# Identity matmuls behind the steps of a delta-rule chain

## The chip, the core and the metric

The kernel runs on one core of one Trainium2 chip. The metric is the device time of one execution, in microseconds. The core has five engines with queues of their own, each of which takes its instructions in the order written: TensorE (PE in the profile, with its weight loads as PEld), VectorE (DVE), ScalarE (ACT), GpSimd (POOL) and SyncE (SP), which here issues the DMAs.

## The reference

The reference is a trunk of four layers over a sequence of 1024 tokens with 1024 channels. The layers' mixers are a gated short convolution (layers 0 and 3), a diagonal state-space scan (layer 1) and RWKV-7 time mixing (layer 2). The change concerns layer 2 alone. Its core is a recurrence over tokens for 16 heads of 64 channels:

```python
def _rwkv_step(state, inp):
    r_t, w_t, k_t, v_t, kk_t, a_t = inp
    sa = jnp.einsum("bhvk,bhk->bhv", state, -kk_t)
    state = (state * w_t[:, :, None, :] + sa[..., None] * (kk_t * a_t)[:, :, None, :]
             + v_t[..., None] * k_t[:, :, None, :])
    out = jnp.einsum("bhvk,bhk->bhv", state, r_t)
    return state, out
```

Around it stand the projections of r, k, v and z, a normalisation by head, and an output projection; each layer ends with a gate and a layer norm.

## The kernel before, in words

Activations lie with channels on the 128 partitions and tokens along the row, in two halves of 512 tokens (h = 0 and 1, "first" and "second half" in this text). Large projections run as three matmuls with a high and a low part of each operand (`mm3`, lines 326 to 328), over eight blocks of 128 input channels: 24 matmuls of 512 columns into one PSUM bank. Their outputs come from the pool `pmm`, which has three banks in this layer. Weights arrive by DMA (L295) and are split by ScalarE (L298) and VectorE (L299).

In the delta-rule layer, channels go in eight pairs of heads, m0 to m7, for each half. The recurrence is done in chunks of 64 tokens, eight chunks to a half. For each pair there are these parts:

- the projection of k and `use_k` (L1708 on), the projection of r and `use_r` (L1750 on): scaling, decay and norms, on all engines;
- `prep`: products within a chunk (L1982, `s`), masks on VectorE, copies on ScalarE, transposes (L2006), more small matmuls (L2017);
- `tsolve`: a triangular solve on VectorE (L2037 to L2054);
- `join`: what the solve gave is brought into the chain's operands (L2076 to L2109);
- `seq`: the chain itself, eight steps that follow each other, and behind them the output with its normalisation (L2141 on).

One step of `seq` is a matmul of the state into a partial sum (L2127), a copy of 64 rows of it by ScalarE (L2128), a second matmul with that copy (L2131), and two instructions on VectorE that decay the state and add the result (L2134). The next step's first matmul needs the new state. All matmuls of the chain are plain fp32 of 128 columns; the trace has two records for each.

The parts are Python generators. Their instructions are written by `pull` between those of the projections: while pair m is projected and prepared, `tsolve` of the pair before and `seq` of the pair before that one are pulled. Besides, a scheduler reorders instructions by priority and readiness when the program is built; `prio` gives `seq`, `tsolve`, `prep` and `join` a priority ahead of their place in the code. So the order on each engine comes from code, priorities and free buffers together. The layer's first half ends with m7, then the projections of the second half's z and v come (about 160 us), then the second half's eight pairs.

Of the kernel before, what the change touches and what calls it, by code (L numbers as in the profile page):

```python
# [8 lines left out]
F32 = mybir.dt.float32  # L9
# [6 lines left out]
P = 128  # L16
NB = 8
T = 1024
HT = 512
# [922 lines left out]
def rsqrt(S, t, y, v):  # L942

    V = S.nc.vector
    V.tensor_scalar(y.bitcast(I32), v.bitcast(I32), -0.5, float(0x5f3759df), ALU.mult, ALU.add)
    V.tensor_scalar(v, v, -0.5, None, ALU.mult)
    for _ in range(3):
        if v.shape[-1] == 1:
            V.scalar_tensor_tensor(t, y, v, y, ALU.mult, ALU.mult)
        else:  # L950
            V.tensor_tensor(t, y, y, ALU.mult)
            V.tensor_tensor(t, t, v, ALU.mult)
        V.scalar_tensor_tensor(y, t, 1.5, y, ALU.add, ALU.mult)
# [574 lines left out]
    w_out_res(S, ("ssm_w_out", (0,)), y2, resid, "b")  # L1528


DECAY = math.exp(-0.5)
GN_EPS = 64e-5
NC = 16
# [52 lines left out]
def rsqrt_small(S, pool, dst, v, n, V):  # L1586

    nc = S.nc
    t = pool.tile([P, n], F32, tag=f"rs_t{n}", name="rs_t", bufs=2)
    nc.scalar.activation(t, v, AF.Ln)  # L1590
    nc.scalar.activation(dst, t, AF.Exp, scale=-0.5)
    V.tensor_tensor(t, dst, dst, ALU.mult)
    V.tensor_tensor(t, t, v, ALU.mult)
    V.tensor_scalar(t, t, -0.5, 1.5, ALU.mult, ALU.add)
    V.tensor_tensor(dst, dst, t, ALU.mult)


def rwkv_layer(S, X, bg, l, last, nxt):
# [102 lines left out]
    def use_k(m, h, ps, R):  # L1701
# [4 lines left out]
        G.memset(pt[:, :, 0:1], 1.0)  # L1706
        SC.activation(pt[:, :, 1:], c3(cs), AF.Exp, scale=-DECAY)
        SC.activation(cs, cs, AF.Exp, scale=DECAY)  # L1708
        R.pc = rg.tile([P, 8], F32, tag="pc", name="pc", bufs=5)
# [212 lines left out]
def inner_setup(S, rg, T_):  # L1922
    nc = S.nc
# [30 lines left out]
    def sq(nm):  # L1954
        return S.pseq.tile([P, HT], F32, tag="sq", name=nm)
# [158 lines left out]
    def seq(m, h, R, dVT, dST, dBV, dZ, dY):  # L2114
        st = rg.tile([P, P], F32, tag="state", name="state", bufs=2)
        if h == 0:
            G.memset(st, 0.0)
        else:
            nc.sync.dma_start(st, dST[m][:])
        ot = S.tmp.tile([P, HT], F32, tag="t_u", name="o")  # L2120
        o4 = ot.rearrange("p (c s) -> p c s", c=4)
        for c in range(8):
            w, c2 = c % 2, c // 2
            rb = rows_b[w]
            uv = R.uv[w][:, c2, :]
            p1 = R.p1[w][:, c2, :]
            nc.tensor.matmul(p1, R.ra[:, c, :], st, start=False, stop=False, skip_group_check=True)  # L2127
            SC.copy(uv[rb, :], p1[rb, :])  # L2128
            yield
            p2 = sq("p2")  # L2130
            last = nc.tensor.matmul(p2[:, 0:P], R.kbt[c // 4][:, c % 4, :], uv, start=True, stop=True)  # L2131
            for hd in range(2):
                cs = slice(hd * 64, hd * 64 + 64)
                V.scalar_tensor_tensor(st[cs, cs], st[cs, cs], R.pc[cs, c:c + 1], p2[cs, cs], ALU.mult, ALU.add)  # L2134
            yield
        with S.tc.issue_after(last.ins):
            for c2 in range(4):
                for hd in range(2):
                    for w in range(2):
                        cs = slice(hd * 64, hd * 64 + 64)  # L2140
                        nc.tensor.matmul(R.p1[w][rows_k[w], c2, cs], R.scr[w][:, c2, hd, :], R.uv[w][:, c2, cs],  # L2141
                                         start=False, stop=True, skip_group_check=True)
        for w in range(2):
            SC.copy(o4[rows_k[w]], R.p1[w][rows_k[w]])
        if h == 0:
            nc.sync.dma_start(dST[m][:], st)

        hs = slice(h * HT, (h + 1) * HT)
        o = ot.rearrange("p (g v) -> p g v", v=64)
        s1 = rg.tile([P, 8], F32, tag="gn_s", name="gn_s", bufs=2)  # L2150
        s2 = rg.tile([P, 8], F32, tag="gn_q", name="gn_q", bufs=2)
        bcs = lambda t: t.unsqueeze(2).to_broadcast([P, 8, 64])
        gsq = S.tmp.tile([P, 8, 64], F32, tag="t_u", name="gsq")
        for g in range(8):
            SC.activation(gsq[:, g, :], o[:, g, :], AF.Square, scale=0.125, accum_out=s2[:, g:g + 1])
        G.tensor_scalar(s2, s2, GN_EPS, None, ALU.add)
        yield
        if m == NB - 1:
            rsqrt(S, rg.tile([P, 8], F32, tag="rs_t8", name="rs_t", bufs=2), s1, s2)
        else:  # L2160
            rsqrt_small(S, rg, s1, s2, 8, V)
        G.tensor_tensor(o, o, bcs(s1), ALU.mult)
        bv = S.tmp.tile([P, HT], F32, tag="ln_s", name="bv", bufs=1)
        nc.sync.dma_start(bv, dBV[m][:, hs])
        z = S.tmp.tile([P, HT], F32, tag="ln_v", name="zz", bufs=1)
        nc.sync.dma_start(z, dZ[m][:, hs])
        ps = sq("otp")
        for i in range(4):
            nc.tensor.transpose(ps[:, i * P:(i + 1) * P], ot[:, i * P:(i + 1) * P], S.ident)
        yt = S.tmp.tile([P, HT], F32, tag="t_u", name="yt")  # L2170
        q4 = lambda ap: ap.rearrange("p (c w t) -> p c w t", w=2, t=CH)
        SC.activation(q4(yt), q4(ps)[:, :, ::-1, :], AF.Identity, scale=gn[:, m:m + 1], bias=bn[:, m:m + 1])
        G.tensor_tensor(yt, yt, bv, ALU.add)
        G.tensor_tensor(yt, yt, z, ALU.mult)
        nc.sync.dma_start(dY[m][:, hs], yt)
        yield
# [29 lines left out]
```

## Time and profile before

| What | Value |
|---|---|
| Runs shown | 2845.06, 2836.07, 2841.19 us |
| Median | 2841.19 us |
| Profiled execution | 2839.38 us, of which the span from first to last instruction 2837.7 us |
| Mean granted clock of TensorE | 0.963 |
| Delta-rule sequences, first half | from 1350.5 us to 1661.0 us |
| Delta-rule sequences, second half | from 1822.7 us to 2109.9 us |

The table of the page gives each engine's busy time and share of the span. Its line PEclk gives the clock granted to TensorE in 40 slices, in tenths of full speed. A row of busy time by stretch reads: start and end, length, then for PE, PEld, DVE, ACT and POOL the busy time and (x) the instructions, then the mean granted clock, the share of time that the DMA engines were busy, and GB/s. A row of the timeline reads: start, length, engine, line, operation, output<-inputs, shape and count; in brackets the idle time of the engine before it, and whose work ended that.

### The profile page before, as it was taken

What the parts mean: (1) busy time and instruction counts of PE and PEld (TensorE: products, weight loads), DVE (VectorE), ACT (ScalarE), POOL (GpSimd) and SP (SyncE); (2) the same over time, 40 slices, a digit from 0 to 9 for tenths busy, and PEclk for the clock granted to TensorE, in tenths of its full rate; (3) what the DMA queues carried; (4) which work ended last, traced back from release to release, by engine and by line L of the source; (5) the groups of instructions that cost most, each with busy time, mean ns of one, the idle gap of its engine ahead of it and who ended that gap; (6) DMA issues with size and microseconds to landing.
All of it is one profiled execution on the core that took longest, in us unless ns stands there. A gap on an engine that the chain in (4) does not pass through costs nothing.

```text
span 2837.7 us, 40655 instructions
## 1 busy us (share of the span) xinstructions
PE 2681.3 (94%) x14939; PEld 2127.4 (75%) x14939; DVE 1994.8 (70%) x3584; ACT 1163.1 (41%) x2211; POOL 646.9 (23%) x696
## 2 busy tenths in 40 slices
PE   8999999999999999899888799898889999999998
PEld 6877788778877888576667567666768777887887
DVE  6787865477657346888888667888756678876544
ACT  3333322242135223656555476555534343224332
POOL 1143422221116132203333110333232211111000
PEclk9999999999999999999997799999699999999999
DMA  5333322347884333473222245223234433324511
GB/s 168 98 97 97 95 75 66 89 142 212 220 240 140 104 94 122 117 233 107 78 85 87 63 151 170 84 91 89 78 100 135 144 111 111 108 71 129 171 64 38
DMA packets 463128, 331.56 MB, mean 117 GB/s; under 512 B 49449, under 2 KB 398929, under 8 KB 462929
## 3 DMA queue, kind: packets, MB, share of 16 engines
q1 hardware_dynamic: 462928, 328.96, 38.3%
q8 instruction: 118, 1.93, 0.3%
q14 instruction: 82, 0.66, 0.1%
HBM read 250.77 MB, written 77.59 MB: 116 GB/s over the span
## 4 chain that ended last, share of the span: by engine, by line
PE 70%; DVE 16%; ACT 4%; issue 4%; DMA 3%; POOL 3%; SPq 0%; DVEq 0%; POOLq 0%; ACTq 0%
PE op L327 3%; PE op L326 3%; PE op L328 3%; PE gp L328 3%; PE gp L327 3%; PE gp L326 3%; PE sp L326 3%; PE sp L327 3%; PE sp L328 2%; DVE tv L2048 2%; PE qa L508 2%; PE qa L506 2%; PE qa L507 2%; PE zp L326 2%; PE zp L328 2%
## 5 line engine op out<-in xcount | busy, mean ns | idle before, releaser
L299 DVE TENSOR_TENSOR wl<-wraw,wh 128x1024 fp32r<-128x1024 f32 x255 | 331.1, 1299 | 217.9 <-ACT wh L298 214.2
L298 ACT CAST wh<-wraw 128x1024 fp32r<-128x1024 f32 x255 | 267.5, 1049 | 517.7 <-PE gp L327 191.5
L905 POOL TENSOR_TENSOR ln_s<-ln_s,rp 128x512 f32<-128x512 f32 x42 | 60.0, 1429 | 209.8 <-DVE rp L901 209.8
L2134 DVE SCALAR_TENSOR_TENSOR state<-state,pc,p 64x64 f32<-64x64 f32 x256 | 71.1, 278 | 46.9 <-PE p L2131 42.1
L2048 DVE TENSOR_TENSOR tv<-ti,mi 128x128 f32<-128x128 f32 (+3 forms) x128 | 97.8, 764 | 2.4
L2127 PE MATMUL p<-state,ra 128*128 128x128 f32 x256 | 65.6, 343 | 28.8 <-DVE state L2134 26.7
L2128 ACT COPY uv<-p 64x128 f32<-64x128 f32 x128 | 33.1, 259 | 136.5 <-PE p L2127 135.8
L2127 PEld LDWEIGHTS p<-state,ra 128*128 128x128 f32 x256 | 45.8, 217 | 54.1 <-DVE state L2134 44.0
L1982 PEld LDWEIGHTS s<-ra,kb 64*128 64x128 f32 x512 | 64.7, 213 | 20.4 <-ACT scr L1988 6.2
L1982 PE MATMUL s<-ra,kb 64*128 64x128 f32 x512 | 75.2, 314 | 4.1 <-DVE kb L1738 1.9
L328 PE MATMUL gp<-r_0h,wl 128*128 128x512 f32 x192 | 77.5, 404 | 0.0
L327 PE MATMUL gp<-r_0l,wh 128*128 128x512 f32 x192 | 76.8, 400 | 0.0
L326 PE MATMUL gp<-r_0h,wh 128*128 128x512 f32 x192 | 76.6, 399 | 0.0
L326 PE MATMUL gp<-r_1h,wh 128*128 128x512 f32 x192 | 76.4, 398 | 0.0
L920 POOL TENSOR_TENSOR rp<-r_0h,r_0l 128x512 f32<-128x512 f32 x24 | 36.3, 1544 | 174.9 <-PE op L327 174.9
L328 PE MATMUL gp<-r_1h,wl 128*128 128x512 f32 x192 | 76.1, 396 | 0.1
L2131 PE MATMUL p<-uv,kbt 128*128 128x128 f32 x256 | 66.8, 347 | 9.9 <-ACT uv L2128 9.8
L327 PE MATMUL gp<-r_1l,wh 128*128 128x512 f32 x192 | 75.6, 394 | 0.0
L2131 PEld LDWEIGHTS p<-uv,kbt 128*128 128x128 f32 x256 | 44.5, 212 | 37.7 <-ACT uv L2128 31.9
L1991 POOL TENSOR_TENSOR scr<-scr,mask 128x512 f32<-128x512 f32 x32 | 46.0, 1436 | 55.4 <-ACT scr L1988 55.2
L326 PE MATMUL sp<-xs0h,wh 128*128 128x512 f32 x128 | 56.1, 438 | 2.6 <-DVE aq L1720 2.2
L327 PE MATMUL sp<-xs0l,wh 128*128 128x512 f32 x128 | 56.0, 437 | 1.9 <-DVE xs0l L195 1.9
(851 smaller groups left out, 8669.6 us busy)
## 6 DMA issues: line engine op xcount, KB each, us to landing
wraw<-in_conv_w_in_dram SPq DMA_DIRECT2D x84, 512.0 KB
wraw<-in_rwkv_w_rkvz_dram SPq DMA_DIRECT2D x64, 512.0 KB
wraw<-in_ple_gate_dram SPq DMA_DIRECT2D x56, 512.0 KB
wraw<-in_conv_w_out_dram SPq DMA_DIRECT2D x24, 512.0 KB
xt<-xd SPq DMA_DIRECT2D x48, 256.0 KB
wraw<-in_ssm_w_in_dram SPq DMA_DIRECT2D x21, 512.0 KB
xd<-rp SPq DMA_DIRECT2D x40, 256.0 KB
wraw<-in_rwkv_w_out_dram SPq DMA_DIRECT2D x16, 512.0 KB
```

Source lines behind the costliest of these rows:

```text
L298: nc.scalar.copy(wh, raw)
L299: nc.vector.tensor_tensor(wl, raw, f32(wh[:]), ALU.subtract)
L326: nc.tensor.matmul(ps, lh, xh, start=(n == 0), stop=False)
L327: nc.tensor.matmul(ps, lh, xl, start=False, stop=False)
L328: nc.tensor.matmul(ps, ll, xh, start=False, stop=(n == kt - 1))
L506: nc.tensor.matmul(ps, wh[:, k0 + k, :], xh, start=first and k == 0, stop=False, skip_group_check=True)
L905: nc.gpsimd.tensor_tensor(s, s, rs, ALU.add)
L1982: nc.tensor.matmul(pss[hd][:, c * P:(c + 1) * P], kb[rows, 2 * c + w, :], ra[rows, 2 * c + w, :], start=True, stop=True)
L2048: V.tensor_tensor(tv, ti[:, b:8, 4 * b:4 * b + 4].unsqueeze(2).to_broadcast([P, n, c, 4]), mi[:, 4 * b:4 * b + 4, 0:c].rearrange("p q c -> ...
L2127: nc.tensor.matmul(p1, R.ra[:, c, :], st, start=False, stop=False, skip_group_check=True)
L2131: last = nc.tensor.matmul(p2[:, 0:P], R.kbt[c // 4][:, c % 4, :], uv, start=True, stop=True)
L2134: V.scalar_tensor_tensor(st[cs, cs], st[cs, cs], R.pc[cs, c:c + 1], p2[cs, cs], ALU.mult, ALU.add)
```

## The change

Nine of the sixteen sequences, named in a table by half and pair (m2 to m6 of the first half, m2 to m5 of the second), take a tile from the pool `pmm`, so one of its three banks, and write matmuls of the 128x128 identity with itself into it. No instruction reads them. One such matmul follows the first matmul of each step, and two follow the second, but for the last step. Dependencies that hold the order on TensorE alone, without a semaphore, tie each to the matmul ahead of it, and tie the chain's next matmul to the last of them. The rest of the code is as it was.

```diff
+WARM = (2, 3, 4, 5, 6), (2, 3, 4, 5)
...
+        warm = S.pmm.tile([P, HT], F32, tag="mm", name="warm") if m in WARM[h] else None
+
+        def then(i, n):
+
+            for _ in range(n if warm is not None else 0):
+                d = nc.tensor.matmul(warm[:, 0:P], S.ident, S.ident, start=True, stop=True)
+                after(d, i)
+                i = d
+            return i
+
+        def after(d, i):
+            if warm is not None and i is not None:
+                S.tc.add_manual_dep(d.ins, i.ins.name, mybir.DependencyInfo(
+                    mybir.DependencyClass.NoSync, mybir.DependencyReason.DATA), reason="order")
+        i = None
         for c in range(8):
...
-            nc.tensor.matmul(p1, R.ra[:, c, :], st, start=False, stop=False, skip_group_check=True)
+            m1 = nc.tensor.matmul(p1, R.ra[:, c, :], st, start=False, stop=False, skip_group_check=True)
+            after(m1, i)
             SC.copy(uv[rb, :], p1[rb, :])
+            i = then(m1, 1)
             yield
             p2 = sq("p2")
             last = nc.tensor.matmul(p2[:, 0:P], R.kbt[c // 4][:, c % 4, :], uv, start=True, stop=True)
+            after(last, i)
+            i = then(last, 2) if c < 7 else None
```

The scheduler orders the whole layer anew around them. On TensorE, in the second half's sequence of m3, a step with the projection's matmuls (`sp`) between its links (`p`) stood so before:

```order
L2131 MATMUL p_17777<-uv,kbt 128x128
L326 MATMUL sp<-xs0h,wh 128x512
L327 MATMUL sp<-xs0l,wh 128x512
L328 MATMUL sp<-xs0h,wl 128x512
L326 MATMUL sp<-xs0h,wh 128x512
L2127 MATMUL p_17609<-state,ra 128x128
L327 MATMUL sp<-xs0l,wh 128x512
L328 MATMUL sp<-xs0h,wl 128x512
L2131 MATMUL p_17783<-uv,kbt 128x128
```

In the changed kernel the same place reads as follows (L2150 and L2144 are the chain's second and first matmul, L2129 the identities):

```order
L2150 MATMUL p_17895<-uv,kbt 128x128
L2129 MATMUL warm<-ident 128x128 x2
L328 MATMUL sp<-xs0h,wl 128x512
L326 MATMUL sp<-xs0h,wh 128x512
L2144 MATMUL p_17748<-state,ra 128x128
L2129 MATMUL warm<-ident 128x128
L327 MATMUL sp<-xs0l,wh 128x512
L2150 MATMUL p_17904<-uv,kbt 128x128
```

Of six projection matmuls in a step three are left, and three identities stand with them; the other projection matmuls of the pair now stand between the sequences.

On ScalarE, before, the preparation of the next pair (`scr`, `pt`, `kp`, `dg`, `kbt`) stood among the chain's copies (`uv<-p`) of that same sequence:

```order
L2128 COPY uv<-p_17609 64x128
L1988 COPY scr<-s_17964 128x4x64
L1707 ACTIVATE pt<-cs 128x8x64
L1718 ACTIVATE kp<-ga,c_om,vec_174 128x512
L1988 COPY scr<-s_17965 128x4x64
L1995 COPY dg<-sca 32x256 x2
L1997 COPY m_17934<-sca 32x256
L1708 ACTIVATE cs<-cs 128x512
L2008 COPY kbt<-kbtp 128x512 x2
L2128 COPY uv<-p_17610 64x128
```

In the changed kernel the copies follow each other, and behind the last of them stand the output's normalisation (`gsq`) and then the preparation:

```order
L2146 COPY uv<-p_17747 64x128
L2146 COPY uv<-p_17748 64x128
L298 CAST wh<-wraw 128x1024
L2165 COPY o<-p_17747 64x512
L2165 COPY o<-p_17748 64x512
L2176 ACTIVATE gsq,gn_q<-o 128x64 x8
L1758 CAST kph<-kp 128x512
L1592 ACTIVATE rs_t<-gn_q 128x8
L1593 ACTIVATE gn_s<-rs_t 128x8
L1990 COPY scr<-s_18101 128x4x64
L2193 ACTIVATE yt<-otp,vec_174 128x512
L1990 COPY scr<-s_18102 128x4x64
```

So the preparation has moved from inside the sequence to behind it; on VectorE the masks (L1986 before) that go with it have moved likewise. The unwarmed sequences have changed as well: the last three steps of m1, in both halves, now stand on TensorE without any matmul between their links.

## The prediction

> **What bounds the kernel now.** I read the page first, then the busy time by stretch over the delta-rule layer, then the timeline inside single steps. The page says that TensorE looks full and that its clock is not always granted:
>
> ```profile
> PE 2681.3 (94%) x14939; PEld 2127.4 (75%) x14939; DVE 1994.8 (70%) x3584; ACT 1163.1 (41%) x2211; POOL 646.9 (23%) x696
> ...
> PEclk9999999999999999999997799999699999999999
> ```
>
> The three slices below 9 lie in the delta-rule layer. So I cut that layer into periods: each row below runs from the last state update (L2134) of one sequence to the last of the next. These are the first half's pairs m2 to m6, then the second half's m2 to m6.
>
> ```profile
> core 0: us, PE busy (x) PEld busy (x) DVE busy (x) ACT busy (x) POOL busy (x), PEclk, DMA share, GB/s
> ...
> 1416.80:1460.00 43.20, 35.18 (x354) 27.07 (x348) 34.06 (x76) 22.50 (x63) 13.92 (x15) 0.96 0.24 76
> 1460.00:1506.40 46.40, 42.15 (x473) 33.43 (x475) 38.23 (x96) 26.85 (x75) 16.82 (x19) 0.89 0.26 74
> 1506.40:1545.00 38.60, 30.79 (x307) 25.63 (x305) 31.99 (x77) 21.09 (x61) 13.72 (x14) 0.73 0.35 115
> 1545.00:1583.70 38.70, 34.90 (x200) 26.28 (x198) 33.12 (x66) 22.15 (x58) 10.71 (x9) 0.78 0.17 52
> 1583.70:1627.00 43.30, 30.24 (x260) 22.59 (x256) 27.37 (x70) 16.86 (x49) 7.32 (x12) 0.62 0.25 72
> ```
>
> ```profile
> 1890.80:1927.40 36.60, 33.27 (x340) 24.57 (x339) 32.15 (x76) 21.91 (x63) 13.59 (x14) 1.00 0.30 90
> 1927.40:1964.00 36.60, 33.02 (x339) 24.47 (x338) 32.12 (x76) 21.91 (x63) 13.57 (x14) 1.00 0.28 89
> 1964.00:2004.90 40.90, 33.51 (x297) 27.09 (x296) 29.88 (x73) 20.22 (x60) 14.34 (x13) 0.65 0.24 67
> 2004.90:2047.30 42.40, 39.08 (x350) 32.46 (x348) 32.84 (x79) 21.31 (x62) 11.03 (x12) 0.65 0.34 108
> 2047.30:2082.70 35.40, 32.52 (x354) 24.34 (x349) 30.33 (x74) 17.61 (x51) 5.18 (x7) 1.00 0.35 109
> ```
>
> Two things are to be seen. At a clock of 1.00 a period takes 36.6 us with VectorE busy for 32.1 of it (88%): there VectorE is the nearest thing to a bound, not TensorE. At a clock of 0.65 the like period takes 40.9 to 42.4 us, 4 to 6 us more, although a third of the clock was missing for all of it. So a lost clock costs, but far less than one for one.
>
> Where the clock goes is plain in the first half's m6, whose steps have nothing beside them:
>
> ```profile
> 1605.00:1610.00 5.00, 2.68 (x13) 1.66 (x11) 3.78 (x8) 2.44 (x5) 2.56 (x2) 1.00 0.45 146
> 1610.00:1615.00 5.00, 1.58 (x5) 1.10 (x6) 4.76 (x11) 0.46 (x2) 0.00 (x0) 0.64 0.91 259
> 1615.00:1620.00 5.00, 2.96 (x9) 1.79 (x8) 3.76 (x11) 0.52 (x2) 0.00 (x0) 0.50 0.07 19
> ```
>
> With 5 matmul records in 5 us the clock falls to half and stays there. One such step, at half clock, from the timeline:
>
> ```profile
> 1616.16 0.79 PE L2127 MATMUL p<-state,ra 128*128 128x128 f32 x2 [0.67 <-DVE state L2134]
> ...
> 1616.99 0.26 ACT L2128 COPY uv<-p 64x128 f32<-64x128 f32 x1 [2.35 <-PE p L2127]
> ...
> 1617.31 0.80 PE L2131 MATMUL p<-uv,kbt 128*128 128x128 f32 x2 [0.35 <-ACT uv L2128]
> 1618.14 0.58 DVE L2134 SCALAR_TENSOR_TENSOR state<-state,pc,p 64x64 f32<-64x64 f32 x2 [0.50 <-PE p L2131]
> ```
>
> and one at full clock, in m5, which has ordinary matmuls between its links:
>
> ```profile
> 1573.47 0.49 PE L2127 MATMUL p<-state,ra 128*128 128x128 f32 x2
> ...
> 1573.72 0.48 PE L326 MATMUL sp<-xs3h,wh 128*128 128x512 f32 x1
> ...
> 1574.00 0.26 ACT L2128 COPY uv<-p 64x128 f32<-64x128 f32 x1 [0.55 <-PE p L2127]
> 1574.03 0.40 PE L328 MATMUL sp<-xs3h,wl 128*128 128x512 f32 x1
> ...
> 1574.32 0.49 PE L2131 MATMUL p<-uv,kbt 128*128 128x128 f32 x2
> ...
> 1574.56 0.48 PE L327 MATMUL sp<-xs3l,wh 128*128 128x512 f32 x1
> ...
> 1574.84 0.59 DVE L2134 SCALAR_TENSOR_TENSOR state<-state,pc,p 64x64 f32<-64x64 f32 x2
> 1574.88 0.39 PE L328 MATMUL sp<-xs3h,wl 128*128 128x512 f32 x1
> ...
> 1575.11 0.39 PE L326 MATMUL sp<-xs3h,wh 128*128 128x512 f32 x1
> ...
> 1575.34 0.40 PE L327 MATMUL sp<-xs3l,wh 128*128 128x512 f32 x1
> ...
> 1575.49 0.19 PEld L2127 LDWEIGHTS p<-state,ra 128*128 128x128 f32 x1 [0.19 <-DVE state L2134]
> ```
>
> The warm step is 1575.49 - 1573.47 = 2.02 us. In the cold one each link's matmul takes 0.80 instead of 0.49, 0.31 twice, so about 2.6 us.
>
> **The change part by part.** *Do the identity matmuls hold the clock?* A sequence adds 8 behind the first matmul of a step and 14 behind the second (none behind the last step's second): 22 in each of 9 sequences, 198. In the warm step the next matmul starts 1573.72 - 1573.47 = 0.25 us after the chain's own, so I price one at 0.25 us of TensorE; the other end is 0.80, a whole one alone at half clock. A bare step holds two such matmuls, 0.5 us in 2.6; with three more it holds 1.25 us in about 2.1, three times the share. The stretch in which the clock fell had a fifth of its time in chain matmuls; the step quoted at full clock had 0.5 and six projection matmuls 0.23 us apart, 1.88 in 2.02 us. 1.25 us alone lies between, and with the three projection matmuls that mostly stay beside it makes 1.94. So I take it that the clock stays at 1.00 in the nine sequences.
>
> [...]
>
> *Do they lengthen a step?* The chain's links stand behind them in TensorE's queue. Between the first matmul and the second lie 1574.32 - 1573.47 = 0.85 us, in which the chain waits for the copy; the changed order puts there the chain's 0.25, one identity (0.25) and one projection matmul (0.23, from 1574.88 to 1575.11): 0.73, hidden. From the second to the next step's first lie 1.17 us; there now stand 0.25 + 2 x 0.25 + 2 x 0.23 = 1.21. So a step costs 0.0 to 0.05 us more, under 0.4 us a sequence. At half clock these sums double and the cover is gone, 0.8 us a step.
>
> *What moves.* The order shows the larger effect. Where two to four projection matmuls of 512 columns stood between two links, one or two now stand, since the identities take their place; and the ScalarE and VectorE work of the next pair's preparation stands behind the sequence instead of inside it. A period becomes two stages: a dense stretch between sequences, then a sequence with little but the triangular solve beside it. The kernel before has one pair that already has that shape, m5 of the first half. Its two stages, then the next pair's (m6), then the second half's m3 (warm) and m4 (cold), each as the stretch between and the sequence:
>
> ```profile
> 1545.00:1567.90 22.90, 20.55 (x111) 15.98 (x107) 18.07 (x34) 15.27 (x43) 10.71 (x9) 0.63 0.19 61
> 1567.90:1583.70 15.80, 14.34 (x89) 10.30 (x91) 15.05 (x34) 6.88 (x16) 0.00 (x0) 1.00 0.12 38
> 1583.70:1606.00 22.30, 19.19 (x214) 15.39 (x208) 9.76 (x26) 13.92 (x41) 5.30 (x9) 0.62 0.17 48
> 1606.00:1627.00 21.00, 11.05 (x47) 7.19 (x48) 17.61 (x44) 2.94 (x9) 2.02 (x4) 0.63 0.34 98
> 1927.40:1938.80 11.40, 10.69 (x170) 8.14 (x169) 9.52 (x30) 7.92 (x32) 2.58 (x4) 1.00 0.06 19
> 1938.80:1964.00 25.20, 22.33 (x171) 16.33 (x169) 22.61 (x48) 14.00 (x32) 11.00 (x11) 1.00 0.38 120
> 1964.00:1974.80 10.80, 8.78 (x157) 6.87 (x157) 8.83 (x27) 7.69 (x31) 2.74 (x4) 0.93 0.07 20
> 1974.80:2004.90 30.10, 24.72 (x142) 20.22 (x141) 21.05 (x46) 12.52 (x30) 11.60 (x10) 0.56 0.30 84
> ```
>
> So sequences shrink from 25 to 30 us to about 17 (15.8 in m5, with a little for the few VectorE instructions that stay), and the stretch between grows from 11.4 to something near m5's 22.9. That one ran at a clock of 0.63 with VectorE busy for 18.07; at full clock I put it between 18.1 (VectorE alone) and 22.9, and take 21.5, since ScalarE now has about 19 us there where m5 had 15.27 (a period's 21.91 less the eight copies of 0.26 and little else). A usual period is then 38.5 us, with ends 35 and 41.
>
> *The sum.* Six sequences get this shape (first half m3, m4, m5; second half m3, m4, m5). Before they took 46.4 + 38.6 + 38.7 + 36.6 + 40.9 + 42.4 = 243.6 us; after 6 x 38.5 = 231, so 12.6 us less. The two m2 lose work that slides to later pairs, and m6 and m7 of each half take it up: VectorE's total is the same, so I count this exchange at nothing, within 8 us either way; m6 of the first half also gets 7 x (2.6 - 2.02) = 4 us back from its bare steps, which I set against the longer queue that it now has. Against that stands a new exposure: in the changed order the unwarmed m1 of both halves ends in three bare steps, which had matmuls beside them; a cold spell there costs up to 3 x 0.6 us in each, so some 2 us in all, between 0 and 3.6. Sum: -12.6 + 2, about -11 us.
>
> *The PSUM bank.* The new tile is one of the three buffers of the pool that the projections use, from its first identity to its last. Two are left to run ahead with; no row shows the pool as a wait, so its cost is what the changed order already shows, at least nothing beyond it, at most one projection's 24 x 0.23 = 5.5 us per half. I take nothing. No engine gets a new semaphore wait: the added dependencies hold between instructions of TensorE alone.
>
> **The rivals.** *A, slower: the stretch between becomes a serial chain through ScalarE.* The projection of the next pair now has to end before its preparation begins, and about 19 us of ScalarE work waits in turn on TensorE, VectorE and POOL. The stretch of m6 (22.3 us with VectorE busy for 9.76, ScalarE 13.92) speaks for it; 11.4 us for 9.52 in the second half's m3 speaks against it. At 25 us a period is 42, six are 252, 8 us more than before, and with 5 for the exchange and 2 for the cold steps the kernel is 15 us slower: 2856. It decides from 23.6 us on, where 23.6 + 17 is the old mean of 40.6.
>
> *B: the identities don't hold the clock.* Then the sequences are as cold as m6 before: 21.0 against 15.8, 5 us in each of nine, less what is cold today already, so some 20 us slower, 2861. Against it: the stretch with 170 matmuls, most of them plain fp32 of small tiles, kept 1.00. [...]
>
> *C, no change: VectorE sets the pace.* The periods at 1.00 are 88% VectorE, and the same VectorE work remains; what the clock returns is then spent waiting for it. The three periods at 1.00 (36.6, 36.6, 35.4) speak for it. It gives 2838 to 2843. [...]
>
> *D, larger gain.* If all nine warmed periods come to the 36.6 us that the warm ones had, 9 x 36.6 = 329.4 replaces 366.7 (the sum of the nine rows), 37 us less: 2804. For it: m2 and m3 of the second half. Against it: the overlap that they have is what the new order gives up.
>
> **How the numbers follow.** The profiled execution took 2839.4 us; the median of the three runs shown is 2841.2, so I add 2 us. Forecast: 2841 - 11 = 2830 us. A chance of 0.38 for it (its own range 2818 to 2838), 0.15 for D, 0.20 for C, 0.22 for A, 0.05 for B. A measurement of this kernel can tell about 0.3% from no change, 8.5 us. Faster by more than that: D and most of the forecast, 0.50. Within: C and the forecast's upper end, 0.22. Slower: A, B and a rest, 0.28. The range from 2802 to 2857 leaves out B and the ends of A and D.
>
> **What would show it.** In the changed profile: a clock of 1.00 in the warmed sequences (if it stays near 0.6, B); steps of 2.0 to 2.1 us there where VectorE has little; sequences of about 17 us and stretches between of 20 to 23 (25 and more is A, with ScalarE or VectorE waiting on each other; 12 to 18 is D); half clock at the end of both m1. The forecast is wrong if the six usual periods sum to more than 243 us.

## The result

The changed kernel takes 2922.9 us (median of four executions, 2920.0 to 2925.3); the kernel before took 2841.7 us beside it (2836.1 to 2845.1). The ratio is 1.0287, with a 95% interval of 1.0268 to 1.0306: 81 us slower, where 11 us faster was forecast. The profiled execution has a span of 2921.6 us (2837.7 before) and a mean granted clock of 0.947 (0.963 before). So the identities, which were to hold the clock, left the kernel with less of it.

### The profile page after: what moved, and what is told of

Same layout as the page of the kernel before. It is cut to its first block, busy times and chain, and to the rows that moved or that the text cites. A ratio compares the mean times of both kernels' runs of the same rounds, so it can differ in the third digit from the quotient of the medians.

```text
span 2921.6 us, 41455 instructions
## 1 busy us (share of the span) xinstructions
PE 2762.0 (95%) x15335; PEld 2211.6 (76%) x15335; DVE 2004.4 (69%) x3584; ACT 1166.1 (40%) x2211; POOL 644.3 (22%) x696
## 5 line engine op out<-in xcount | busy, mean ns | idle before, releaser
L2050 DVE TENSOR_TENSOR tv<-ti,mi 128x128 f32<-128x128 f32 (+3 forms) x128 | 90.1, 704 | 2.8
L2144 PE MATMUL p<-state,ra 128*128 128x128 f32 x256 | 65.9, 344 | 25.1 <-DVE state L2155 16.6
L2144 PEld LDWEIGHTS p<-state,ra 128*128 128x128 f32 x256 | 45.9, 217 | 56.9 <-DVE state L2155 44.4
L2150 PE MATMUL p<-uv,kbt 128*128 128x128 f32 x256 | 66.6, 346 | 6.3 <-ACT uv L2146 5.5
L2129 PE MATMUL warm<-ident 128*128 128x128 f32 x396 | 72.4, 294 | 0.0
L2150 PEld LDWEIGHTS p<-uv,kbt 128*128 128x128 f32 x256 | 44.9, 213 | 33.6 <-ACT uv L2146 27.4
L2129 PEld LDWEIGHTS warm<-ident 128*128 128x128 f32 x396 | 61.2, 211 | 0.1
```

What stands on the lines that cost most here:

```text
L2050: V.tensor_tensor(tv, ti[:, b:8, 4 * b:4 * b + 4].unsqueeze(2).to_broadcast([P, n, c, 4]), mi[:, 4 * b:4 * b + 4, 0:c].rearrange("p q c -> ...
L2129: d = nc.tensor.matmul(warm[:, 0:P], S.ident, S.ident, start=True, stop=True)
L2144: m1 = nc.tensor.matmul(p1, R.ra[:, c, :], st, start=False, stop=False, skip_group_check=True)
```

## The profile after

The page of the changed kernel, the rows of TensorE and of its clock:

```profile
PE 2762.0 (95%) x15335; PEld 2211.6 (76%) x15335; DVE 2004.4 (69%) x3584; ACT 1166.1 (40%) x2211; POOL 644.3 (22%) x696
...
PEclk9999999999999999998688799968789999999999
```

TensorE is busy for 81 us more, VectorE and ScalarE for nearly as long as before (2004.4 and 1166.1 against 1994.8 and 1163.1). The clock is missing in nine slices of the delta-rule layer, against the three of before.

Busy time by stretch, cut as in the prediction into the stretch between two sequences and the sequence: first half m3, m4, m5, and the stretch of m6; then second half m3, m4, m5, and the stretch of m6.

```profile
core 0: us, PE busy (x) PEld busy (x) DVE busy (x) ACT busy (x) POOL busy (x), PEclk, DMA share, GB/s
1459.70:1492.10 32.40, 26.70 (x270) 22.54 (x265) 18.38 (x38) 19.74 (x53) 12.99 (x15) 0.78 0.30 98
1492.10:1509.80 17.70, 17.25 (x121) 13.89 (x122) 13.76 (x38) 2.40 (x8) 0.00 (x0) 0.92 0.02 4
1509.80:1541.40 31.60, 27.20 (x272) 22.36 (x267) 18.05 (x34) 19.12 (x52) 13.15 (x15) 0.78 0.28 86
1541.40:1558.50 17.10, 16.36 (x121) 12.46 (x122) 14.62 (x42) 3.02 (x9) 0.00 (x0) 1.00 0.12 32
1558.50:1590.40 31.90, 26.25 (x273) 21.99 (x268) 18.25 (x37) 19.45 (x53) 12.98 (x15) 0.79 0.49 153
1590.40:1608.00 17.60, 17.15 (x119) 13.93 (x120) 13.80 (x39) 2.69 (x9) 0.00 (x0) 0.90 0.14 29
1608.00:1645.60 37.60, 24.92 (x241) 20.97 (x236) 30.75 (x53) 28.61 (x69) 12.68 (x14) 0.59 0.21 65
...
1966.70:1989.00 22.30, 20.96 (x259) 17.02 (x254) 15.29 (x38) 17.43 (x50) 11.32 (x11) 0.92 0.15 46
1989.00:2006.10 17.10, 15.60 (x118) 12.10 (x118) 13.61 (x35) 3.49 (x10) 1.27 (x1) 1.00 0.30 85
2006.10:2037.10 31.00, 25.27 (x266) 20.80 (x263) 20.65 (x40) 18.16 (x52) 13.20 (x14) 0.84 0.34 105
2037.10:2054.80 17.70, 17.47 (x122) 14.34 (x123) 12.52 (x36) 3.02 (x9) 0.00 (x0) 0.89 0.01 1
2054.80:2087.30 32.50, 26.84 (x269) 22.70 (x264) 18.34 (x37) 19.70 (x53) 12.83 (x14) 0.76 0.32 96
2087.30:2105.80 18.50, 18.06 (x124) 15.08 (x124) 13.84 (x38) 2.44 (x9) 0.00 (x0) 0.87 0.04 7
2105.80:2141.80 36.00, 32.67 (x258) 25.84 (x255) 22.33 (x40) 18.66 (x53) 10.92 (x10) 0.69 0.44 142
```

The sequences are 17 to 18.5 us long at a clock of 0.87 to 1.00, as forecast. The stretches between are 31 to 32.5 us long (22.3 only in the second half's m3), where 21.5 was forecast. Their clock is 0.76 to 0.84 (0.92 in that m3): in these pairs the half clock has moved from the sequences into the stretches. The six usual periods sum to 50.1 + 48.7 + 49.5 + 39.4 + 48.7 + 51.0 = 287.4 us, 44 more than the 243.6 of before.

Cut in the same way over all pairs, m1 to m7 of both halves take 628.8 us (543.4 before), 85 more. The six usual periods give 44 of these; m6 gives 39 (59.6 and 57.9 us, before 43.3 and 35.3); m7 gives 7 and m1 5; m2 gives 9 back. Summed in the same cuts, the clock that is missing (time times the share not granted) is 124 us against 78 before. The loss of time does not follow it: the six usual periods miss 43 us of clock (53 before) and are 44 us longer, while m1 and m2 of both halves miss 55 us (2 before) and are together 4 us shorter.

What fills a stretch now? Before, these matmuls of the preparation and of the join (`kbtp`, `wps`; `zp`, `tp`) stood inside a sequence; the groups of TensorE in the first half's sequence of m4, 1520.6 to 1545.0 us:

```profile
L2017 PE MATMUL wps<-uv,sca 64*64 64x64 f32 x32 | 1.8, 240 | 0.0
L2084 PE MATMUL tp<-tt,t 32*32 32x32 f32 x32 | 1.4, 238 | 0.0
L2006 PE MATMUL kbtp<-ident,kb 128*128 128x128 f32 x4 | 1.1, 421 | 0.0
L2076 PE MATMUL zp<-t,m 32*32 32x32 f32 x32 | 1.1, 237 | 0.4 <-DVE t L2068 0.4
```

In the changed kernel no group of that kind is left in the sequence of m4 (1541.4 to 1558.5 us). All stand in the stretch ahead of it:

```profile
L2019 PE MATMUL wps<-uv,sca 64*64 64x64 f32 x32 | 3.6, 316 | 0.0
L2008 PE MATMUL kbtp<-ident,kb 128*128 128x128 f32 x8 | 2.5, 441 | 3.3 <-POOL kb L2003 2.6 <-ACT kbt L2010 0.7
L2086 PE MATMUL tp<-tt,t 32*32 32x32 f32 x32 | 1.9, 237 | 0.0
L2078 PE MATMUL zp<-t,m 32*32 32x32 f32 x32 | 1.8, 237 | 0.0
```

There they stand one behind another. The timeline of the end of that stretch, TensorE and ScalarE:

```profile
1525.51 1.12 PE L2008 MATMUL kbtp<-ident,kb 128*128 128x128 f32 x4 [2.60 <-POOL kb L2003]
1526.66 0.58 ACT L2010 COPY kbt<-kbtp 128x512 f32<-128x512 f32 x1 [1.78 <-PE kbtp L2008]
1527.30 0.90 PE L2008 MATMUL kbtp<-ident,kb 128*128 128x128 f32 x3 [0.68 <-ACT kbt L2010]
...
1530.72 0.58 ACT L2023 COPY uv<-wps 64x512 f32<-64x512 f32 x1 [0.88 <-PE wps L2019]
1531.96 1.74 PE L2078 MATMUL zp<-t,m 32*32 32x32 f32 x31
...
1533.05 0.36 ACT L2081 COPY t<-zp 32x256 f32<-32x256 f32 x1 [0.41 <-PE zp L2078]
...
1535.10 0.75 ACT L2089 COPY tt<-tp 32x256 f32<-32x256 f32 x2
...
1535.60 2.00 PE L2102 MATMUL p<-uv,tt 64*64 64x64 f32 x29 [0.26 <-ACT tt L2089]
...
1538.65 0.65 ACT L2111 COPY ra<-a 128x256 f32<-128x256 f32 x2 [1.74 <-PE a L2108]
...
1539.07 0.51 PE L2144 MATMUL p<-state,ra 128*128 128x128 f32 x2 [0.30 <-ACT ra L2111]
```

First come the transposes and products of the preparation, which belong to the pair after (`kbtp` with its copy `kbt`, `wps` with `uv`), then those of the join, which the next chain needs: `zp` and its copy `t`, `tp` and `tt`, the products of L2102 and L2108 and the copy `ra`. Each is a round trip from TensorE to ScalarE, the join's by its data and all by their place in the two queues, and the brackets show where one engine waits for the other. Only behind the last of them can the chain begin (L2144). This takes 1539.07 - 1525.51 = 13.6 us. Ahead of it lie 15.7 us with the rest of the projection and the first half of the preparation, as busy time by stretch has it:

```profile
1509.80:1525.50 15.70, 12.55 (x86) 9.27 (x80) 7.43 (x14) 10.11 (x34) 8.52 (x10) 1.00 0.51 151
1525.50:1539.10 13.60, 12.36 (x169) 10.88 (x169) 8.44 (x19) 8.03 (x16) 3.54 (x6) 0.50 0.08 27
```

So the chain's first matmul comes 29.3 us behind the end of the sequence before it. In the kernel before that took 3.4 us in m4, 4.9 in m5 and 6.3 to 6.9 in the second half's m3 to m5 (from the timeline; 12.9 in the first half's m3). The whole serial part runs at half clock, though TensorE shows as busy for 12.36 of 13.6 us.

## The experiments

All were timed in three rounds beside the kernel before, which took 2834.97 to 2837.02 us there. No instruction reads an identity's result, so none of the edits changes what is computed. "Periods" below are the sum of m1 to m7 of both halves, "missing clock" the clock missing in them (before: 543.4 and 78 us).

### The step's own bank in place of the third bank

```diff
-        warm = S.pmm.tile([P, HT], F32, tag="mm", name="warm") if m in WARM[h] else None
+        warm = m in WARM[h] or None
...
-                d = nc.tensor.matmul(warm[:, 0:P], S.ident, S.ident, start=True, stop=True)
+                d = nc.tensor.matmul(p2[:, P:2 * P], S.ident, S.ident, start=True, stop=True)
...
-            i = then(m1, 1)
-            yield
             p2 = sq("p2")
+            i = then(m1, 3)
+            yield
...
-            i = then(last, 2) if c < 7 else None
+            i = None
```

> The same nine sequences, but all three identities of a step stand behind its first matmul and write into the unused columns of the bank that the step's second matmul will use; no bank of the projections' pool is taken. 9 x 24 = 216 identities. In the built order the next pair's preparation stays inside the sequence, as before the change (ScalarE work between two sequences 7 to 14 us by mean durations, VectorE 13 to 16, against 20 and 19 in the changed kernel). Theory 'order' (the time is lost because the preparation moved behind the sequence): 2815 to 2850 us. Theory 'bank' (the projections wait for the bank that the identities hold): 2815 to 2850 as well. Theory 'TensorE time' (the identities' own time delays what stands behind them): 2880 or more.

Measured: 2857.62 us, 1.0073 [1.0058, 1.0088]; periods 564.4, missing clock 55. This lies 8 us above the range of the first two theories and 22 us below that of the third. Most of the loss is gone with the bank, but 0.7% stays, though 23 us of clock came back.

### The same three identities in the third bank

```diff
-            i = then(m1, 1)
+            i = then(m1, 3)
...
-            i = then(last, 2) if c < 7 else None
+            i = None
```

> As the run with the step's own bank, the same three identities at the same place behind the first matmul, but written into a bank of the projections' pool, as in the change. In the built order the preparation stands behind the sequence (ScalarE 18 us between sequences, 3 within). Theory 'order': 2890 to 2930 us, most of the change's loss. Theory 'bank': 2890 to 2930. Theory 'TensorE time': the same as the run with the step's own bank, 2880 or more both.

Measured: 2899.58 us, 1.0227 [1.0204, 1.0251]; periods 601.5, missing clock 101. The two kernels have the same identities behind the same matmul, and differ in the bank that they are written to. That costs 42 us. The groups of TensorE show where they go. In the run with the step's own bank, first half, inside the sequence of m4 (1524.6 to 1550.9 us):

```profile
L2008 PE MATMUL kbtp<-ident,kb 128*128 128x128 f32 x8 | 1.9, 420 | 0.0
L2019 PE MATMUL wps<-uv,sca 64*64 64x64 f32 x32 | 1.5, 223 | 0.0
L2086 PE MATMUL tp<-tt,t 32*32 32x32 f32 x32 | 0.9, 193 | 0.0
```

and in the run with the third bank, in the stretch ahead of that sequence (1503.5 to 1528.8 us):

```profile
L2086 PE MATMUL tp<-tt,t 32*32 32x32 f32 x32 | 1.7, 215 | 0.4 <-ACT t L2081 0.4
L2019 PE MATMUL wps<-uv,sca 64*64 64x64 f32 x32 | 1.3, 221 | 0.0
...
L2008 PE MATMUL kbtp<-ident,kb 128*128 128x128 f32 x8 | 1.1, 280 | 1.5 <-POOL kb L2003 1.5
```

With these identities in a bank held through the sequence, the scheduler puts the preparation and the join behind it; with a bank that the step has anyway, they stay beside the steps. The clock differs as well (55 against 101 us missing), so the 42 us are the price of the new order with the clock that it loses. The changed kernel, with two of the three identities behind the second matmul, is at 1.0287; where that further 0.6% arises was not taken apart.

### The bank held, nearly no identities

```diff
-                d = nc.tensor.matmul(warm[:, 0:P], S.ident, S.ident, start=True, stop=True)
+                d = nc.tensor.matmul(warm[:, 0:2], S.ident, S.ident[:, 0:2], start=True, stop=True)
...
-            i = then(m1, 1)
+            i = then(m1, 1) if c in (0, 7) else None
...
-            i = then(last, 2) if c < 7 else None
+            i = None
```

> The bank is taken and held through the sequence by one matmul of two columns in the first step and one in the last; the other identities are left out. The built order keeps the preparation inside the sequence for the most part (ScalarE 7 to 13 us between, 8 to 21 within). Theory 'order': 2835 to 2870 us, near the kernel before. Theory 'bank': 2890 to 2930, since the hold is the same. Theory 'TensorE time': 2841, as before. The clock should dip in the sequences as before.

Measured: 2872.94 us, 1.0127 [1.0107, 1.0148]; periods 585.1, missing clock 126. This is 3 us above the range of 'order' and outside the two others. Holding the bank by two small matmuls a sequence costs 36 us: nothing here holds the clock, and the order changes again (for m2 to m6 the stretches are 13 to 23 us, the sequences 22 to 30). How much of this belongs to the bank and how much to the ties of its first and last step isn't told apart.

### All identities and the bank, no ties

```diff
-            if warm is not None and i is not None:
+            if False:
```

> All 198 identities and the bank, but without the dependencies that tie them to the steps; in the built order they stand in clumps ahead of and inside the sequences, and the preparation stays inside (ScalarE 7 to 12 us between, 8 to 18 within). Theory 'order': 2840 to 2875 us, what 198 x 0.21 us costs where it isn't covered at the most. Theory 'bank': 2890 to 2930. Theory 'TensorE time': 2885 or more.

Measured: 2837.85 us, 1.0009 [0.9999, 1.0018]; periods 550.2, missing clock 41. Without the ties the scheduler writes the identities in clumps. The rows of the identities alone (TensorE, then its weight loads) in the stretch and the sequence of the second half's m4:

```profile
1974.20:1984.70 10.50, 4.48 (x28) 3.59 (x28) 1.00 0.13 38
1984.70:2008.30 23.60, 0.00 (x0) 0.00 (x0) 1.00 0.29 98
```

So the bank is held briefly and the preparation stays where it was. The time is 2 us below the range of 'order' and far below the two others: neither the identities' time on TensorE nor the tile as such is the loss of 81 us. The run returns 37 us of clock and gains nothing; as the identities take time too (4.48 us for the 14 above), it shows only the sum of the two, not what either is worth.

### The step's own bank, identities of two columns

```diff
-                d = nc.tensor.matmul(p2[:, P:2 * P], S.ident, S.ident, start=True, stop=True)
+                d = nc.tensor.matmul(p2[:, P:P + 2], S.ident, S.ident[:, 0:2], start=True, stop=True)
```

(as a change to the first experiment)

> The run with the step's own bank, with its 216 identities cut to two columns: the ties, the place and the earlier hold of the step's bank stay, the identities' time and their hold on the clock go. That run lost 0.7% against the kernel before, with the clock lost for 55 us in all periods against 79. Theory 'identities' time' (the 216 x 0.2 us lengthen steps or push other work): 2825 to 2843 us, the loss gone. Theory 'new order' (any change of the chain's code makes the scheduler write an order that overlaps worse): 2850 to 2865, the loss stays. The clock should be lost for more than in that run.

Measured: 2887.53 us, 1.0178 [1.0157, 1.0199]; periods 589.0, missing clock 109. Both theories missed it. Cutting the identities short makes the kernel 30 us slower than with whole ones. ScalarE's work stands as in the first experiment (within 1.2 us in each stretch and sequence of the first half's m3 to m5), VectorE's within 5 us; the large difference is twice the missing clock, with three tied matmuls in each step all the same. If the clock is what makes the difference, it is worth about half its size here: 25 us of periods for 54 us of clock.

### The step's own bank, one identity

```diff
-            i = then(m1, 3)
+            i = then(m1, 1)
```

(as a change to the first experiment)

> One identity of full width behind the first matmul of each step of the nine sequences, in the step's own bank. The built order is all but that of the kernel before (VectorE and ScalarE work between and within sequences differ by 1 us at most in twelve of fourteen pairs). Theory 'clock is worth something when the order stays': 2815 to 2830 us, by 10 to 20 us of 79 lost. Theory 'VectorE sets the pace, and the clock is worth nothing': 2832 to 2845.

Measured: 2838.14 us, 1.0001 [0.9988, 1.0014]; periods 539.7, missing clock 65. The order stays almost that of before, 13 us of clock come back, and there is no change to be measured.

### Identities in the stretch too

```diff
+    def idents(t):
+        for _ in range(4):
+            nc.tensor.matmul(t[:, 0:P], S.ident, S.ident, start=True, stop=True)
+        return t
...
-            ps = aux("kbtp")
+            ps = idents(aux("kbtp"))
```

(the like ahead of `wps`, `zp`, `tp` and `a2`, in their own banks: 24 a pair)

> The changed kernel with 24 more identities in each of the sixteen pairs' preparation and join, ahead of the transposes and small matmuls there and in the banks that these use, so that the clock is held in the stretch between sequences as well. In the built order VectorE work between sequences rises to 24 us (from 19) and falls to 7 within; ScalarE stays at 20 and 1. Theory 'half clock in the stretch' (the stretch is 22 us long at full clock, and 31 because the clock falls there): stretches of 23 to 27 us, the whole 2850 to 2885. Theory 'order alone' (the chain through ScalarE and VectorE takes 31 us at any clock): 2920 to 2960.

Measured: 2905.57 us, 1.0247 [1.0225, 1.0269]; periods 614.5, missing clock 32. The stretch of the first half's m4, and its serial part alone (from the first transpose to the chain's first matmul):

```profile
1503.90:1535.40 31.50, 27.36 (x322) 22.13 (x316) 21.99 (x47) 19.24 (x53) 13.00 (x15) 1.00 0.33 103
...
1519.50:1532.20 12.70, 9.84 (x203) 8.61 (x202) 11.85 (x26) 7.50 (x16) 4.49 (x6) 1.00 0.22 70
```

The whole falls between the two theories. At full clock the stretch is as long as in the changed kernel with half clock in its serial part, 31.5 against 31.6 us, and the serial part takes 12.7 against 13.6 us. But here the identities stand in the serial chain themselves: in each of the groups `wps`, `zp`, `tp` and `a` their eight records run ahead of the matmuls that the chain needs. For `tp`, with the copies that it reads:

```profile
1526.39 0.75 ACT L2086 COPY t<-zp 32x256 f32<-32x256 f32 x2 [0.62 <-PE zp L2083]
...
1526.80 1.16 PE L1958 MATMUL tp<-ident 128*128 128x128 f32 x8 [0.45 <-ACT t L2086]
...
1527.89 0.69 PE L2091 MATMUL tp<-tt,t 32*32 32x32 f32 x32
```

The copies end at 1527.14, and the matmuls that read them start 0.75 us later, 1.09 us behind the first identity. Over the four groups this makes 2.7 us counted from the end of the copies, 4.4 us counted from the first identity. So without them the serial part would take 8.3 to 10.0 us at full clock, and the stretch 27 to 29 us (estimates). Half clock is a part of what makes the stretch long, but not the larger one. VectorE, too, has 4 us more of work in this stretch than in the changed kernel.

### Twelve identities a pair in the stretch

The same with three identities ahead of each `kbtp`, `zp` and `tp` alone.

> The changed kernel with three more unread identities ahead of each of the four tiles kbtp, kbtp, zp and tp of every pair, in those tiles' own banks: 12 a pair, 192 in all. The built order keeps nearly the same VectorE work between the sequences of the usual pairs (by mean durations 21, 19 and 21 us against 19, 18 and 19 in the changed kernel; the run with 24 identities a pair had 24), so this tells the stretch's clock from its order better than that run did. Theory 1, the stretch between is a serial chain whose length the clock hardly sets: the clock of the stretches of m3, m4 and m5 rises to 0.9 or more, they stay at 30 to 32 us, and the kernel takes 2900 to 2925 us. Theory 2, half clock makes the stretch long: with the clock back, the 7 us of clock that each stretch lacks come back for the most part, stretches of 25 to 27 us, and with some nine of them the kernel takes 2860 to 2880 us. Between 2880 and 2900 both have a part.

Measured: 2898.05 us, 1.0217 [1.0200, 1.0235]; periods 606.3, missing clock 75. The total falls between the two theories. The stretches of the first half's m3 and m4, and the serial part of m4:

```profile
1455.10:1486.30 31.20, 27.62 (x297) 22.99 (x292) 19.50 (x42) 19.14 (x52) 13.09 (x15) 0.89 0.32 104
...
1504.40:1530.20 25.80, 21.93 (x289) 18.26 (x284) 18.24 (x38) 17.81 (x51) 13.67 (x14) 1.00 0.33 106
...
1515.80:1528.00 12.20, 10.23 (x195) 8.84 (x195) 11.04 (x23) 8.86 (x19) 6.78 (x7) 1.00 0.20 66
```

With half of the missing clock back, m3 is 1.2 us shorter than in the changed kernel. m4 became 5.8 us shorter, but mostly in its part ahead of the transposes, where no clock was missing in the changed kernel either: 11.4 us in place of 15.7, in an order that differs there; nine of the projection's matmuls stand in the serial part instead, for one. The serial part went from 13.6 to 12.2 us with these nine and 18 records of identities inside it. The changed kernel itself has a better pair to compare: the same part, without identities, in its second half's m4, with half of the missing clock back:

```profile
2021.20:2033.20 12.00, 9.46 (x168) 8.35 (x168) 11.02 (x21) 7.55 (x17) 4.73 (x5) 0.75 0.23 68
```

That is 1.6 us less than at 0.50. With the estimate from the run before, half clock costs some 3 to 5 us of the 13.6, and 8 to 10 would stay at full clock (estimates).

### Four identities a pair in the stretch

The same with two identities ahead of each `kbtp` alone.

> The changed kernel with two unread identities ahead of each of the two tiles kbtp of every pair: 4 a pair, 64 in all. In the first half the built order of VectorE and ScalarE between and within the sequences of m3, m4 and m5 is that of the changed kernel by mean durations (19 and 12 us on VectorE, 20 and 1 on ScalarE). Theory 1, serial chain: if the clock rises in some of these stretches, they stay at 31 to 32 us; the kernel takes 2910 to 2925 us. Theory 2, half clock: a stretch whose lost clock falls by some us becomes shorter by nearly as much; if these few identities do not hold the clock, the kernel stays at 2920 us and says nothing.

Measured: 2915.06 us, 1.0272 [1.0248, 1.0296]; missing clock 106. These few don't hold the clock: the stretches of the first half's m3 to m5 have 0.76 to 0.83 and are 33.8 to 34.8 us long. The run says nothing on the clock's worth; it is a miss.

### The kernel before with identities in the stretch

The functions of the run with 24, with two identities at each place, in the kernel before: 12 a pair, no ties and no third bank.

> The kernel before, without any identity in the sequences, with 12 identities in each pair's preparation and join (two ahead of each group, 192 in all), in banks that these groups use anyway; no ties and no bank of the projections' pool. The built order keeps the overlap of the kernel before. Theory 'clock is worth something when the order stays': 2815 to 2830 us. Theory 'VectorE sets the pace': 2832 to 2845. Theory 'any identity costs its time': 2860 or more (192 x 0.2 = 38 us at the most).

Measured: 2831.09 us, 0.9993 [0.9978, 1.0009]; periods 548.0, missing clock 56. This lies between the ranges of the first two theories. Clock comes back, 22 us of it, and no time that can be measured; again this is the sum of clock and identities.

### The changed kernel with another priority, and its control

```diff
-PS, PT, PJ = 300, 300, 600
+PS, PT, PJ = 100, 300, 600
```

PS is what the scheduler gives the sequences ahead of their place in the code. In the changed kernel:

> The changed kernel whole, with all 198 identities, their ties and the third bank held, but the sequences' priority in the scheduler is 100 instead of 300 (PS). In the built order the preparation and the join of the next pair then stand inside the sequence again: ScalarE's work between and within the sequences of m3, m4, m5 of the second half is, by mean durations, 9 and 13, 8 and 13, 8 and 16 us, where the changed kernel has 18 and 2, 20 and 1, 20 and 1 (the kernel before 8 and 13, 9 and 11, 7 and 14). The first half is between the two (18 and 5, 15 and 11, 7 and 19). Theory 1, the loss is the place of the preparation and the join, a serial chain of TensorE and ScalarE that nothing covers once it stands alone: most of the loss goes, 2835 to 2865 us, with second-half stretches of 12 to 17 us. Theory 2, the identities and the bank cost their time wherever the preparation stands: 198 identities at 0.25 us and the projection held back by one bank, 2885 us or more. Between 2865 and 2885 both have a part.

In the kernel before:

> The kernel before with the sequences' priority at 100 instead of 300 and nothing else: the control for the run of the changed kernel with that priority. In its built order ScalarE's work between and within the sequences is as in the kernel before (8 and 14, 7 and 13, 8 and 12 us against 8 and 13, 8 and 13, 9 and 11 for the second half's m2 to m4). So 2825 to 2850 us is expected by both theories. If it is below 2825 us, the priority is worth something by itself, and the other run is to be compared with this one and not with the kernel before.

Measured: the changed kernel 2861.09 us, 1.0080 [1.0062, 1.0098], periods 575.2, missing clock 78; the kernel before 2867.39 us, 1.0107 [1.0091, 1.0123], periods 596.4, missing clock 118. The changed kernel's stretches and sequences of the second half's m4 and m5:

```profile
1987.10:2003.80 16.70, 13.35 (x153) 11.11 (x152) 14.18 (x35) 9.57 (x33) 6.75 (x6) 0.90 0.16 45
2003.80:2030.00 26.20, 25.44 (x234) 20.66 (x233) 17.32 (x43) 12.41 (x29) 6.63 (x9) 1.00 0.31 96
2030.00:2045.60 15.60, 12.25 (x149) 10.22 (x148) 14.17 (x34) 9.52 (x33) 6.17 (x6) 0.93 0.10 28
2045.60:2073.70 28.10, 26.11 (x233) 21.77 (x231) 23.74 (x50) 15.54 (x35) 7.62 (x7) 0.92 0.58 184
```

All 198 identities, all ties and the held bank are still there, and the loss is 24 us in place of 81. Stretch and sequence have the shape of before, with ScalarE's work inside the sequence, and the chain's first matmul comes 5.7 us into the stretch again. The control rules out that the priority itself brings this: it makes the kernel before 30 us slower, which the expectation (2825 to 2850) had not seen and which was not taken apart. With that priority the change makes the kernel no slower; it is 6 us faster, 0.2%, and each of its four executions (2856.3 to 2862.0) is below each of the control's (2865.3 to 2870.4). Its periods are 21 us shorter than the control's, and most of that is given back ahead of the first period, between the halves and behind the last. No version here beats the kernel before by more than can be measured.

## Why the prediction was wrong

**Held: the clock in the sequences.** Forecast 1.00 and 17 us; measured 0.87 to 1.00 and 17.1 to 18.5 us. Where it is below 1.00, the lost part lies at the start: in these four sequences the first 2.0 us have 0.50, and what follows has 0.91 to 0.98. Rival B is out.

**Held nearly: the steps.** From the third on, the steps of the six usual sequences take 2.0 to 2.7 us in the changed kernel's timeline (the first two are longer); in the timeline of the first half's m3, the longer ones (2.55 to 2.59 us) have VectorE at work on the solve (0.39 to 0.72 us for one instruction of L2050), and in the one of 2.08 us VectorE waits 0.88 us for TensorE. No term of the loss comes from there; a warmed sequence as a whole is about as long as forecast.

**Failed: "what moves".** The step that failed is "the stretch between grows from 11.4 to something near m5's 22.9 ... and take 21.5". Five of six measured 31.0 to 32.5. The model for it, m5 of the kernel before, held `s` and products of the join (L2100) but no `kbtp`, `wps`, `zp` or `tp`: those stood beside the sequence ahead of it. The prediction saw in the changed order that the preparation had moved, added ScalarE's 4 us of it, and counted it as work on an engine. But preparation and join together are five round trips one behind another, and no chain is left to stand beside them: 11.7 to 14.0 us from the first transpose to the chain's first matmul in the six pairs, at clocks of 0.50 to 0.88. That is more than the 10 us between 21.5 and 31 to 32. The same step put the stretch at full clock, though no identity stands in its serial part; five of six had 0.76 to 0.84. This is the smaller part: the estimate at full clock, 27 to 29 us, is still well over 21.5. For the six usual periods the step makes 287 where 231 was forecast.

**Failed with it: the exchange "at nothing, within 8 us either way".** m2, m6 and m7 together came out 37 us longer, almost all in m6, whose stretches hold the serial chain and the work that slid there: 37.6 us with VectorE busy for 30.75, and 36.0. With the lower priority the two m6 fell from 117.5 to 73.5 us (before 78.6), which points to the order here too.

**Failed: the PSUM bank at nothing.** "No engine gets a new semaphore wait" was beside the point. The bank acts when the program is ordered: held from a sequence's first step to its last by tied identities, it costs 42 us against the same identities in the step's own bank. Bank and ties together do most of it: ties without the bank cost 0.7%, the bank without ties nothing that can be measured (1.0009, with the clock that came back).

**Right in kind, wrong in size: rival A.** A serial chain through ScalarE was named as the danger, with a chance of 0.22, and priced at 25 us a stretch and 15 us in all. The stretch that spoke for it, the first half's m6 of the kernel before (22.3 us), did hold the whole serial chain, from the first transpose to the chain's first matmul:

```profile
1584.72 1.07 PE L2006 MATMUL kbtp<-ident,kb 128*128 128x128 f32 x8 [0.60 <-ACT scr L1988]
...
1604.34 0.49 PE L2127 MATMUL p<-state,ra 128*128 128x128 f32 x2
```

These 19.6 us, with 13 matmuls of the projection among them, hold no `s`, while m5's stretch holds `s` and not the chain. So the prediction had both parts of the new stretch in its rows, and took each for a model of the whole. A's own sign, stretches of 25 us and more, came: 31.0 to 32.5 in five of six.

**Too small: the bare steps of m1.** Forecast 0 to 3.6 us in all; the two m1 are 5 us longer. Their last steps take 2.6 us at half clock, as priced, but the clock is lost over nearly the whole of both m1 (0.54 and 0.57, before 1.00), not in their last steps alone.

**What the clock is worth.** The prediction put a lost clock at 4 to 6 us a period. Where the order stayed near that of before, 13, 22 and 37 us of clock came back and no time with it (1.0001, 0.9993 and 1.0009); each of these runs gives only the sum of what the clock brings and what its identities cost. In two pairs of runs with orders that are alike, though not the same, clock was worth about half its size: 25 us of periods for 54 us of clock in the step's own bank, 21 for 40 with the lower priority. No run that kept the old order came to the forecast's 11 us. TensorE's busy time rose from 2681.3 to 2762.0 us with the change, and the kernel became 81 us slower.

**Open.** Why a held bank makes the scheduler place the preparation behind the sequence isn't shown, only that it does, and that a lower priority of the sequences undoes it. The share of ties and bank in the run that held the bank with two small matmuls is open. With the lower priority the first half's periods stay 20 us over those of before (305.4 against 285.0), m4 most (50.0 against 38.6); that rest was not taken apart. How much of a stretch's length half clock makes is an estimate, since no run here had its serial part at full clock without identities or other added work in it.

## What to carry to other kernels

When a change moves work, list what the new place must do one thing behind another, and price it as a chain of round trips at the clock that it will get, not by an engine's busy time; a stretch taken as a model must hold the same operations. A filler for which its engine has room can still cost the order (42 us between two banks here): give it no buffer that others rotate through, and compare the built order on the engines that fill the gaps. Before buying clock, check by one small run that clock is what the time waits for, and count what the fillers themselves take.

## What was not expected of the hardware

- The granted clock was 0.50 through a stretch in which TensorE shows as busy for 12.36 of 13.6 us (169 matmul records, 160 of them of 32x32 and 64x64), and 1.00 in the same part of the run with 24 identities a pair, with 203 records of which 34 are identities, busy for 9.84 of 12.7 us. Here TensorE's busy time did not tell whether the clock held: 91% went with 0.50, and 77% with 1.00.
- That serial part took 13.6 us at 0.50 and 12.0 us at 0.75 in the same kernel; at 1.00 it would take an estimated 8 to 10 us (from the 12.7 us of the run with 24 identities a pair, less 2.7 to 4.4). By this estimate doubling the clock would not halve it.
- 198 identities (396 records of 0.275 us) in clumps, with 37 us of clock that came back, left the time as it was: 1.0009 [0.9999, 1.0018].
